# A first load of 64 KB rows, issued as a 2 KB strip of each row and then the other 62 KB

## Chip, cores, metric

One core of one Trainium2 chip. The metric is the device time of one execution in microseconds; the profile's span (first to last instruction of the program) is about 1.8 us shorter than that time. "Before" and "changed" are always compared on the same chip, in alternating rounds.

## The reference

The kernel turns 96 float32 images of 256 by 256 by 180 degrees. No arithmetic: each image's 65,536 elements come out in reverse order.

```python
def setup_inputs():
   batch, c, h, w = 32, 3, 256, 256
   return {"x": np.random.randn(batch, c, h, w).astype(np.float32)}

def reference(x: np.ndarray) -> np.ndarray:
   return np.rot90(x, k=2, axes=(-2, -1)).astype(np.float32)
```

## The kernel before

The 96 images are cut into three groups of 32, and each image into 4 pieces of 64 KB, so that a group fills a tile of 128 partitions by 64 KB. A load is one transfer of 128 rows of 64 KB. VectorE reverses each row inside SBUF (from tile A to tile C in four copies, or within tile B in twelve), and the store writes the four pieces of an image in reverse order. All transfers are issued by the sync engine, and they stand in one queue (q1, with all 864 packets of the page).

```python
    A = pool.tile([P, E], x.dtype, tag="A")        # E = 16384 elements, 64 KB
    Bt = pool.tile([P, E], x.dtype, tag="B")
    Ct = pool.tile([P, E], x.dtype, tag="C")
    T = pool.tile([P, J], x.dtype, tag="T")
    ...
    def load(t, g, lo=0, hi=E):
        nc.sync.dma_start(out=t[:, lo:hi], in_=x4[g][:, lo:hi])

    def store(t, g):
        nc.sync.dma_start(out=o4[g][:, ::-1, :], in_=t[:, :])

    def across(dst, src):
        for c in range(0, E, K):                   # K = E // 4
            copy(dst[:, c:c + K], back(src, E - c - K, E - c))
    ...
    load(A, 0)
    load(Bt, 1)
    across(Ct, A)
    store(Ct, 0)
    load(A, 2)
    inside(Bt)
    store(Bt, 1)
    across(Ct, A)
    store(Ct, 2)
```

Of the kernel before, what the change touches and what calls it, by code (L numbers as in the profile page):

```python
# [2 lines left out]

os.environ.setdefault("NEURON_RT_ULTRASERVER_MODE", "4")

# [4 lines left out]


@with_exitstack
def kernel(
    ctx: ExitStack,
    tc: tile.TileContext,
    x: bass.AP,
    out: bass.AP,
):








    nc = tc.nc
    P = 128

    B, C, H, W = x.shape
    L = H * W
    G = 32
    E = L // 4
    K = E // 4
    J = E // 8

    x4 = x.rearrange("b c h w -> (b c) (h w)").rearrange(
        "(g n) (s e) -> g (n s) e", n=G, s=4)
    o4 = out.rearrange("b c h w -> (b c) (h w)").rearrange(  # L40
        "(g n) (s e) -> g n s e", n=G, s=4)

    pool = ctx.enter_context(tc.tile_pool(name="slots", bufs=1))
    A = pool.tile([P, E], x.dtype, tag="A")
# [4 lines that stand above are left out]
    def back(t, lo, hi):  # L49
        return t[:, hi - 1:(lo - 1 if lo else None):-1]  # L50

    def copy(dst, src):
        tc.keep_in_program_order(nc.vector.tensor_copy(out=dst, in_=src))  # L53
# [8 lines that stand above are left out]
        for c in range(0, E, K):  # L62
            copy(dst[:, c:c + K], back(src, E - c - K, E - c))

    def inside(t):
        for lo in range(0, E // 2, J):
            hi = E - lo - J
            copy(T[:, :], back(t, hi, hi + J))
            copy(t[:, hi:hi + J], back(t, lo, lo + J))
            copy(t[:, lo:lo + J], T[:, :])  # L70

    load(A, 0)
    load(Bt, 1)
    across(Ct, A)
    store(Ct, 0)
# [7 lines that stand above are left out]
# [1 line left out]
_INS = ['x']  # L84
_OUTS = [((32, 3, 256, 256), 'float32')]


# [23 lines left out]
```

## Time and profile before

| | before |
|---|---|
| time, median of 3 runs | 123.19 us (123.14 to 123.35) |
| span in the profile | 121.3 us |
| share of the DMA queue | 97.3% |
| VectorE busy | 32.5 us |

The lines behind this table, and what they say, stand in the prediction. Some words for what follows: a transfer "lands" when the last of its 16 semaphore increments, one by each engine, has arrived (96 in the trace, for six transfers). The trace also has a record for each packet (start, duration, bytes), one packet for each row of a transfer and one for each increment; where I speak of "the packet records", the figures are worked out from those. The "loss" of a packet is the time that it takes over the steady duration of packets of its size (2.418 us for 64 KB), given per engine as a mean over the 16.

### The profile page before, as it was taken

Reading aid. Unit: us, or ns where it says so; the run is one execution under the profiler, and the core shown is the slowest. Engines: PE = TensorE matmul, PEld = TensorE weight load, DVE = VectorE, ACT = ScalarE, POOL = GpSimd, SP = SyncE. Lnnn points to the kernel's source line nnn. Section 1 sums busy time; section 2 is a strip of 40 time slices with the busy share of each in tenths; the row PEclk is TensorE's granted clock in tenths of the full one; section 3 lists DMA queues with packets and bytes.
Section 4 is the critical chain, followed back from the end, with each engine's and each line's share of the span. In section 5 each row is a group of like instructions: output and inputs, shape, how many; then the busy total and the mean of one; then the engine's idle time right before and its main releaser. Section 6 shows DMA issues by size and latency. Waiting matters only on the chain.

```text
span 121.3 us, 72 instructions
## 1 busy us (share of the span) xinstructions
DVE 32.5 (27%) x20; POOL 0.2 (0%) x4
## 2 busy tenths in 40 slices
DVE  0000000599300079999100000009990000000000
POOL 0000000000000000000000000000000000000000
DMA  9777977997899497799789977997798779877980
GB/s 346 346 346 346 692 346 346 389 649 346 346 432 605 195 497 346 346 605 432 346 346 605 432 346 346 627 411 346 346 649 389 346 346 649 389 346 346 670 368 0
DMA packets 864, 50.33 MB, mean 415 GB/s; under 512 B 96, under 2 KB 96, under 8 KB 96
## 3 DMA queue, kind: packets, MB, share of 16 engines
q1 hardware_dynamic: 864, 50.33, 97.3%
HBM read 25.17 MB, written 25.17 MB: 415 GB/s over the span
## 4 chain that ended last, share of the span: by engine, by line
DMA 59%; DVE 13%; DVEq 2%; SPq 1%; issue 0%
DMA A<-in_x_dram 59%; DVE Ct L53 13%; DVEq L106 2%; SPq L59 1%; DVEq L53 0%
## 5 line engine op out<-in xcount | busy, mean ns | idle before, releaser
L53 DVE COPY Ct<-A 128x4096 f32<-128x4096 f32 x8 | 17.8, 2288 | 46.3 <-DMA A<-in_x_dram 46.3
L53 DVE COPY T<-Bt 128x2048 f32<-128x2048 f32 x4 | 4.9, 1228 | 11.7 <-DMA Bt<-in_x_dram 11.6
L53 DVE COPY Bt<-Bt 128x2048 f32<-128x2048 f32 x4 | 4.9, 1227 | 0.1
L53 DVE COPY Bt<-T 128x2048 f32<-128x2048 f32 x4 | 4.9, 1226 | 0.1
L95 POOL MEMSET const-bfloat16-1.0<- 128x1 bf16 x1 | 0.1, 102 | 0.0
L95 POOL MEMSET const-uint8-127<- 128x1 uint8 x1 | 0.1, 101 | 0.0
L95 POOL MEMSET const-float32-0.0<- 128x1 f32 x1 | 0.1, 99 | 0.2 <-issue 0.2
L95 POOL MEMSET const-float32-1.0<- 128x1 f32 x1 | 0.1, 98 | 0.0
## 6 DMA issues: line engine op xcount, KB each, us to landing
A<-in_x_dram SPq DMA_DIRECT2D x2, 35.7
out_dram<-Ct SPq DMA_DIRECT2D x2, 30.3
Bt<-in_x_dram SPq DMA_DIRECT2D x1, 41.9
out_dram<-Bt SPq DMA_DIRECT2D x1, 42.9
```

The source lines that it names most:

```text
L53: tc.keep_in_program_order(nc.vector.tensor_copy(out=dst, in_=src))
L59: nc.sync.dma_start(out=o4[g][:, ::-1, :], in_=t[:, :])
L95: nc = _bacc.Bacc("TRN2", target_bir_lowering=False, num_devices=1)
L106: with _tile.TileContext(nc) as tc:
```

## The change

The intent, as far as the code tells it: a small piece first, so that something is there early.

```diff
+    N = E // 32
 ...
-    load(A, 0)
+    load(A, 0, 0, N)
+    load(A, 0, N, E)
     load(Bt, 1)
     across(Ct, A)
```

## The prediction

The forecast's sum came to +0.1 us: 0.05 for eight more packets per engine, 0.01 for one more semaphore packet, and 0.05 for a gap between strip and rest. This last term is cut in step 5 with its reason, which no trace here shows; it was the author's estimate. Without it the sum is +0.06 us, 123.25 in place of 123.3 us.

The 27.2 GB/s per engine and the 6 ns per packet, with which the text reckons, can be worked out from the records of before: a packet of 64 KB takes 2.4155 us from start to start and one of 4 bytes 6 ns, so the bytes alone need 2.4095 us, 27.2 GB/s. "Such packets", 96 of them, are those of 4 bytes, the semaphore increments (the page: 96 under 512 B).

> **What bounds the kernel now.** I read the page first: the busy shares, then the slices, then the queue. They show a core that moves data and does little else.
>
> ```profile
> span 121.3 us, 72 instructions
> DVE 32.5 (27%) x20; POOL 0.2 (0%) x4
> ...
> DMA  9777977997899497799789977997798779877980
> ...
> q1 hardware_dynamic: 864, 50.33, 97.3%
> HBM read 25.17 MB, written 25.17 MB: 415 GB/s over the span
> ```
>
> VectorE is busy a quarter of the span. The one DMA queue is busy 97.3% of it, so only 2.7% of 121.3 us, 3.3 us, is time in which the 16 engines have no packet. The slices swing between 7 and 9 because a packet is 64 KB and its bytes are booked at one moment; they are not idle time.
>
> Next, the chain of waits that ended last. It goes through the first load, the four copies of it, the issue of the store and of the third load, and then the third load's landing. It tells of semaphores and not of the queue: the 49.66 us "wait" for the third load is mostly that load standing in line behind the second load and the first store.
>
> ```profile
> 0.73 21.82 DMA A<-in_x_dram
> 22.55 0.02 issue
> 22.57 8.91 DVE Ct L53 x4
> ...
> 32.17 49.66 DMA A<-in_x_dram
> ```
>
> What shows whether the line ever runs dry is the timeline of the issuing engine, against the landings.
>
> ```profile
> 0.73 0.38 SPq L56 DMA_DIRECT2D A<-in_x_dram  x1
> 1.17 0.42 SPq L56 DMA_DIRECT2D Bt<-in_x_dram  x1
> 31.50 0.63 SPq L59 DMA_DIRECT2D out_dram<-Ct  x1
> 32.17 0.59 SPq L56 DMA_DIRECT2D A<-in_x_dram  x1
> 58.22 0.55 SPq L59 DMA_DIRECT2D out_dram<-Bt  x1
> 90.86 0.54 SPq L59 DMA_DIRECT2D out_dram<-Ct  x1
> ```
>
> ```profile
> DVE Ct L53 <- DMA A<-in_x_dram: 46.3, 2, 23.7
> DVE T L53 <- DMA Bt<-in_x_dram: 11.6, 1, 11.6
> ```
>
> Landings, worked out as issue plus time to landing: first load 0.73 + 21.82 = 22.55; second load 43.09 (VectorE begins on it then, after waiting 11.6 us); first store 31.50 + 31.1 = 62.6; third load 32.17 + 49.66 = 81.8; second store 58.22 + 42.9 = 101.1; last store 90.86 + 29.6 = 120.5. The first store was issued at 31.50 while the second load ran until 43.09, so it had 11.6 us in hand; the last store was issued at 90.86 and its turn came at 101.1, 10.2 us in hand. The queue never waits for VectorE. Each transfer is 8.39 MB, and the landings lie 20.5, 19.5, 19.2, 19.3 and 19.4 us apart.
>
> So the span is a sum: six transfers of about 19.33 us (116.0), plus a start of 22.55 - 19.33 = 3.2 us, plus 1.2 us that the second load takes more than the others, plus 121.3 - 120.5 = 0.8 us after the last landing: 121.2. Only the 3.2 and the 1.2 are not plain streaming.
>
> The trace's packet records give more of both. An engine takes eight 64 KB packets per transfer, one 2.418 us, and the next begins at the end of the one before (mean distance of starts in the middle of the trace: 2.4155 us). The first packets start between 1.74 and 2.70 us (mean 1.95) and end between 4.89 and 5.30 (mean 5.04), so they take 0.67 us more than a later one. Those that start early take up to 3.3 us, the two that start last 2.60: they end together, as if data flowed from about 2.5 us on for all. The other loss is in the last packet of the second load, just before the first store: 3.3 to 4.0 us instead of 2.418, mean loss 1.12. No later change of direction costs more than 0.02 us on average.
>
> [...] the stretch from 3 to 20 us shows 432 GB/s.
>
> ```profile
> 3.00:20.00 17.00, 0.00 (x0) 0.00 (x0) 1.00 1.00 432
> ```
>
> [...] At 27.2 GB/s per engine 65,536 bytes need 2.409 us; with 2.4155 measured, a packet costs 6 ns beside its bytes[...].
>
> [...] The trace has 96 such packets (6 transfers by 16 engines). In the records each takes 9 ns, and the next data packet starts 6 ns after it did[...].
>
> [...]
>
> **The change part by part.** Removed: one issue of 128 rows of 64 KB. Added: an issue of 128 strips of 2 KB and one of 128 rests of 62 KB. The bytes are the same. The static order of instructions shows the rest: the first copy of the first tile now waits for the long part, the fourth copy for the strip, and the third load waits for both; nothing else moves. VectorE's instructions keep their count and size.
>
> 1. Bytes: 0 us.
> 2. Packets: per engine 8 more, at 6 ns: 0.05 us. By rows: 8 x (2048 B / 27.2 GB/s + 6 ns) = 8 x 81 ns = 0.65 us for the strips, 8 x (63,488 B / 27.2 + 6 ns) = 8 x 2.340 = 18.72 for the rests, together 19.37 against 8 x 2.4155 = 19.32. This lies on the path, as everything in the queue does.
> 3. One more semaphore packet per engine: 6 to 9 ns, on the path.
> 4. One more issue on the sync engine: 0.38 to 0.42 us by the timeline, plus 0.06 between. It delays the issue of the rest to about 1.17 and of the second load to about 1.65. The second load has until 22 us, so for it nothing comes of this.
> 5. A gap between strip and rest. If the first packets flow from about 2.5 us, the strips are done at 2.5 + 0.65 = 3.15, for the last engine at about 3.5. The rest, issued 0.44 later than the strip, should have its first packets at 1.74 + 0.44 = 2.2 to 2.70 + 0.44 = 3.1. So they are there in time. [...]
> 6. The waits of VectorE: the long part lands last, at about 22.6, as the whole did; a delay of 0.1 us is eaten by the 11.6 us in hand.
> 7. The start itself: the strip meets the same first-packet delay of 0.67 us, and the rest doesn't pay it again if it is a delay of the first access. 0 us.
>
> Sum: 0.05 + 0.01 + 0.05 = about +0.1 us, a tenth of a per cent: 123.3 us.
>
> **The rivals.** A: small packets are not pipelined, and each strip pays a part of the 0.67 us that the first packet pays. Eight times 0.67 would be 5.4 us, 128.6 us, slower by 4%. Against it: everywhere after the first, packets follow each other without a gap, and the 9 ns semaphore packets too. For it: no data packet below 64 KB of this queue is in the trace. A mild form (0.1 us more per strip) gives +0.8 us, 124.1.
>
> B: the second issue has its own start-up, so that between strip and rest the engines stand still for up to a first-packet delay: +0.5 to +0.9 us, 123.8 to 124.1. For it: the strip is over in about 0.65 us, shorter than the 1.0 us from an issue's start to its first packet. Against it: the rest is issued only 0.44 us later.
>
> C: a gain. The early engines hold their first packet 0.7 us too long; if what delays them depends on the size of the first packet, short ones could hide it: up to -0.7 us, 122.5. Or the 1.12 us stall before the first store depends on how the engines stand to each other or on the count of packets before it, and the strip moves or removes it: 122.1. Against it: the engines' spread is the same after any split, and the first store comes at the same place in the order. Both together make 1.8 us, 1.5%, so even this rival stays within 2%; more than the 3.3 us without a packet plus the two stalls is not there to be won.
>
> D: the copies of the first tile start earlier, because part of the tile is there early. Ruled out by the order of waits: the first copy waits for the long part. Even if it did start earlier, the queue has no use for it.
>
> **Range and chances.** Working point 123.3. Downwards rival C in part, upwards rival B and the mild form of A; runs of one kernel agree within 0.2 us (123.14 to 123.35). Range 122.6 to 124.0. A gain over 2% needs 2.5 us, of which the profile shows no source: 0.01. A loss over 2% needs 0.31 us per strip, the strong rival A: 0.03. Within 2%: 0.96.
>
> **What would show it right or wrong.** In the changed trace: 864 + 128 + 16 = 1008 packets, the same MB; a span of about 121.4; the queue's share near 97%; landings still 19.2 to 19.5 us apart, with the second load's 1.2 extra still there; VectorE's wait for the second load near 11.6. Strips should take about 0.08 us each after the first, and the first long packets should start as the strips end. Wrong would be: strips of several tenths each (A), a stretch between 2.5 and 5 us in which the queue is idle (B), a first landing before 22.2 or a second load nearer to 19.3 (C).

## The result, and the profile after

Changed kernel: 122.98 us median of 4 runs (122.82 to 123.28), before 123.16 (123.02 to 123.35). The ratio is 0.9987 with a 95% interval of 0.9963 to 1.0011: the same. Later, on another chip with five rounds, the same pair gave 1.0008 (0.9996 to 1.0020).

The page of the changed kernel: the span, VectorE, the busy tenths of the DMA engines, the packets and the queue.

```profile
span 121.2 us, 75 instructions
DVE 32.5 (27%) x20; POOL 0.2 (0%) x4
...
DMA  9977987997899497799789977997798779877980
...
DMA packets 1008, 50.33 MB, mean 415 GB/s; under 512 B 112, under 2 KB 112, under 8 KB 240
...
q1 hardware_dynamic: 1008, 50.33, 97.4%
```

1008 packets are the 864 of before, 128 strips and 16 more semaphore increments (112 in place of 96); bytes, share and VectorE stand as before.

The chain of waits (start, duration, what). It has one piece more, the issue of the strip, and then goes the same way with the same lengths.

```profile
0.73 0.38 SPq L58
...
1.17 21.43 DMA A<-in_x_dram
...
22.63 8.91 DVE Ct L55 x4
...
32.31 49.42 DMA A<-in_x_dram
```

The timeline of the issuing engine and VectorE's waits. The second load is issued at 1.63 in place of 1.17 us; its turn comes at 22. VectorE has 11.5 us in hand before the second tile lands, before 11.6.

```profile
0.73 0.86 SPq L58 DMA_DIRECT2D A<-in_x_dram  x2
1.63 0.43 SPq L58 DMA_DIRECT2D Bt<-in_x_dram  x1
31.56 0.63 SPq L61 DMA_DIRECT2D out_dram<-Ct  x1
```

```profile
DVE Ct L55 <- DMA A<-in_x_dram: 46.3, 2, 23.7
DVE T L55 <- DMA Bt<-in_x_dram: 11.5, 1, 11.5
```

The issues with time to landing, in the changed kernel: the strip has landed 2.8 us after its issue, 19 us before the rest, and nobody asks for it then.

```profile
A<-in_x_dram SPq DMA_DIRECT2D x1, 7936.0 KB, 21.4
A<-in_x_dram SPq DMA_DIRECT2D x1, 256.0 KB, 2.8
```

The packet records show the start in detail. Each column is a mean over the 16 engines.

| | before | changed | changed, second profile |
|---|---|---|---|
| first long packet of an engine starts | 1.95 us | 2.94 | 2.85 |
| packets of the first 10 us: time over their steady duration, sum per engine | 0.67 | 0.57 | 0.52 |
| first packet of the second load starts | 21.95 | 21.92 | 21.95 |
| last packet of the second load: time over 2.418 us | 1.12 | 1.13 | 1.33 |
| last packet of all ends | 119.70 | 119.71 | 119.90 |

The third line is the balance of the change: nothing, within 0.03 us, which is less than the noise of that reading (below). The difference between the first and the second profile of the same kernel lies in the fourth line, which the change does not touch.

### The profile page after: what moved, and what is told of

It is laid out like the page before. It is cut to its first block, busy times and chain, and to the rows that moved or that the text cites. A ratio compares the mean times of both kernels' runs of the same rounds, so it can differ in the third digit from the quotient of the medians.

```text
span 121.2 us, 75 instructions
## 1 busy us (share of the span) xinstructions
DVE 32.5 (27%) x20; POOL 0.2 (0%) x4
## 2 busy tenths in 40 slices
DMA packets 1008, 50.33 MB, mean 415 GB/s; under 512 B 112, under 2 KB 112, under 8 KB 240
## 3 DMA queue, kind: packets, MB, share of 16 engines
q1 hardware_dynamic: 1008, 50.33, 97.4%
## 4 chain that ended last, share of the span: by engine, by line
DMA 58%; DVE 13%; DVEq 2%; SPq 1%; issue 0%
DMA A<-in_x_dram 58%; DVE Ct L55 13%; DVEq L109 2%; SPq L61 1%; SPq L58 0%; DVEq L55 0%
## 5 line engine op out<-in xcount | busy, mean ns | idle before, releaser
L55 DVE COPY T<-Bt 128x2048 f32<-128x2048 f32 x4 | 4.9, 1227 | 11.6 <-DMA Bt<-in_x_dram 11.5
```

The source lines that it names most:

```text
L55: tc.keep_in_program_order(nc.vector.tensor_copy(out=dst, in_=src))
```

## The experiments

All kernels were correct. An execution over 1.5% above the fastest of its kernel counts as slow and is left out of a ratio; there was one such in e5 (125.38 us, the fastest 123.04) and one in e6 (124.87, the fastest 122.77). The diffs that take out `load(A, 0, 0, N)` are against the changed kernel, that of e11 is against e6, and the others are against the kernel before.

| run | edit | median us, before beside it | ratio to before (95%) |
|---|---|---|---|
| after_again | the change | 123.17, 123.06 | 1.0008 (0.9996 to 1.0020) |
| e1_strip_last | strip after the rest | 123.24, 123.06 | 1.0018 (1.0001 to 1.0035) |
| e3_halves | two halves | 123.13, 123.06 | 1.0009 (0.9997 to 1.0021) |
| e2_32_strips | 32 strips | 125.17, 123.06 | 1.0167 (1.0154 to 1.0181) |
| e4_strip_64b | strip of 64 bytes | 123.59, 123.27 | 1.0005 (0.9965 to 1.0045) |
| e5_late_second | second load at 4.3 us | 123.20, 123.27 | 0.9990 (0.9943 to 1.0037) |
| e6_early_store | strip stored early, other queue | 122.93, 123.27 | 0.9955 (0.9916 to 0.9995) |
| e7_load_first | third load before first store | 122.92, 123.26 | 0.9976 (0.9958 to 0.9994) |
| e8_second_at_18 | second load at 18.6 us | 123.95, 123.26 | 1.0059 (1.0034 to 1.0084) |
| e9_8_strips | 8 strips | 123.14, 123.23 | 1.0003 (0.9983 to 1.0023) |
| e10_16_strips | 16 strips | 123.44, 123.23 | 1.0018 (1.0005 to 1.0031) |
| e11_store_between | strip stored between loads | 122.84, 123.23 | 0.9967 (0.9952 to 0.9981) |

Differences of 0.1 us cannot be read from these times; they are read from the packet records, which exist once per kernel. Kernels that start with the same undivided load (before, e5, e7, e8) begin their second load at 21.95, 21.87, 21.98 and 21.96 us; this, some 0.05 us to either side, is the noise of that reading.

### Is it the split, or the short packets in front?

The change once more; the strip last; two halves.

> The changed kernel again, for the noise of its trace and a narrower interval. Theory M: ratio 1.000 to 1.001. Rival C: ratio 0.998 to 0.999, and the start's loss again about 0.1 us smaller than before.

```diff
-    load(A, 0, 0, N)
-    load(A, 0, N, E)
+    load(A, 0, 0, E - N)
+    load(A, 0, E - N, E)
```

> The first load is split as in the change, but the 62 KB part of each row comes first and the 2 KB strip last, so the same 1008 packets and issues, with no short packet at the start. Theory M (mine: a split costs 6 ns a packet and a semaphore, about 0.06 us, and where the strip stands does not matter): within 0.1 us of the changed kernel, and the start of the trace loses its 0.67 us as before. Rival C (short first packets take part of the start's delay away, which gives back the 0.06): here the gain is gone, the second load begins 0.1 us later than in the changed kernel, at about 22.0 from the span's start, against 21.90 there and 21.95 before.

```diff
-    load(A, 0, 0, N)
-    load(A, 0, N, E)
+    load(A, 0, 0, E // 2)
+    load(A, 0, E // 2, E)
```

> The first load as two halves of 32 KB of each row: two transfers, but no short packet. Theory M: as the changed kernel, +0.06 us. Rival C (what helps at the start is that the first packets are short): the start's loss is nearer to the 0.67 us of before than to the 0.57 us that the changed kernel's records show.

Measured start of the second load: 21.95 us with the strip in front, 21.97 with the strip last, 21.85 with halves. Loss in the first 10 us: 0.52, 0.63 and 0.52. The first two agree with the theory that only the sum of bytes, packets and semaphores counts. The halves, with packets of 32 KB in front, have as small a loss as the strips, so a gain that only short packets bring is not seen. Over all the runs, the six kernels with 62 to 64 KB packets in front (or with 64 bytes before them) lose 0.60 to 0.68 us, the five with 2 KB or 32 KB in front 0.51 to 0.58, and the one with 8 KB 0.61 (those cut into 4 KB or 2 KB throughout lose 0.92 and 0.99, spread over several transfers). So 0.1 us may be there to be won, the smallest form of rival C, but it does not go by length, and the starts of the second load do not show it beyond their noise. No run settles whether it is real.

### Must the strip have a certain length?

Rival G has the long packets slow at the start whatever strip went before them.

```diff
-    load(A, 0, 0, N)
-    load(A, 0, N, E)
+    load(A, 0, 0, 16)
+    load(A, 0, 16, E)
```

> The strip is 64 bytes of each row in place of 2 KB. Its 8 packets per engine are over in under 0.2 us. Theory M (the delay at the start belongs to the first access, the rest does not pay it again): the long packets that follow lose next to nothing, the total is as in the changed kernel. Rival G [...]: the long first packets show 0.3 to 0.7 us over 2.41 each, as they did in the changed kernel (0.35), and the total is as before. Rival B (a gap because the strip is over before the rest is there): engines idle 0.2 to 0.5 us, second load begins at 22.1 to 22.4.

The chain of waits of this kernel: the whole first tile is there at 23.25 us, in the changed kernel at 22.61.

```profile
1.17 22.08 DMA A<-in_x_dram
23.25 0.02 issue
23.27 8.91 DVE Ct L55 x4
```

The records say why. The 64-byte packets take 8 to 11 ns each and lose nothing at all. Then the engines have nothing until the rest's first packets come, on average at 2.45 us, 0.50 us after an undivided load's would (1.95). Those long packets lose 0.65 us each, as if no strip had gone before. The second load begins at 22.42, 0.47 us later than before. So rival B's gap is real, and it fits the second issue: the rest is issued 0.44 us later, its packets come 0.50 us later, and the load ends as much later. In the changed kernel the 2 KB strips hold the engines for 0.99 us (0.65 at their steady pace and 0.34 of loss), which covers that time. And step 7 falls: the loss at the start is not a first access that a small packet can take on itself.

The whole-execution ratio, 1.0005, doesn't show the half microsecond: its interval is 0.4% to either side, and the runs of before in that batch ran from 122.98 to 124.55.

### Does the second load's issue slow the first packets?

The kernel before, with

```diff
+    nc.gpsimd.memset(Bt[:, 0:4096], 0.0)
     load(Bt, 1)
```

Of rival G this run tests one form: that the early issue of the second load slows the first packets.

> The kernel before, with one change: a memset on GpSimd of a quarter of the second tile makes the second load's issue late by several us (it has until 22 us). [...] Theory M (first access): the start's loss stays 0.67 us, the time is that of before. Rival G [...]: the first packets' mean excess falls from 0.67 to 0.3 us or less, and the time falls by as much, 0.3%.

The second load was issued at 4.27 us, and the first packets still lost 0.60 us (before: 0.67). So it is not the early issue of the second load that slows them. The first load was issued at 0.73 us as before, so whether its own issue slows them stays open.

The records hold a pattern that goes further. Add to the mean start of the first long packets their loss: that is the time from which they would have run at full pace.

| first long packets | issued | start | loss | full pace from |
|---|---|---|---|---|
| undivided load, or 62 KB first (before, e1, e5, e7, e8) | 0.73 us | 1.94 to 1.99 | 0.60 to 0.68 | 2.54 to 2.65 |
| behind a strip of 64 bytes (e4) | 1.17 | 2.45 | 0.65 | 3.10 |
| behind a strip of 2 KB (changed twice, e6, e11) | 1.17 | 2.85 to 2.94 | 0.23 to 0.31 | 3.16 to 3.18 |

The later the rest starts, the less it loses, and it comes to full pace at nearly the same time, some 0.5 us after an undivided load. It looks as if each long transfer had a delay of its own, counted from its issue (1.8 to 2.0 us from there to full pace); no run moved that issue alone, so this is not shown. It would explain the balance of the change: the rest is at full pace 0.54 us later than an undivided load (3.16 against 2.62), the strips have by then brought bytes that take 0.60 us at the steady rate, and the added packets cost about as much as the difference. Why a long transfer starts slowly, I did not find.

### The dose

32, 8 and 16 transfers in place of one.

```diff
-    load(A, 0, 0, N)
-    load(A, 0, N, E)
+    for lo in range(0, E, N):        # e9: 4 * N, e10: 2 * N
+        load(A, 0, lo, lo + N)
```

> The dose: the first load as 32 transfers of a 2 KB strip each, 256 packets per engine in place of 8, and 31 more semaphores. Theory M: 256 x 80 ns = 20.5 us + 31 x 6 ns = 0.2 against 19.3, so +1.3 us, all of it in the first load, the first landing of the whole tile at about 23.9; time about 1.1% above before. Rival A (short packets each pay a latency): several us more than that. Rival B (each transfer has a start of its own, a few tenths): 31 x 0.3 = +9 us. A third: the sync engine's issues, 32 x 0.44 = 14 us, would bind only if an issue took over 0.66 us.

> The first load as 8 transfers of 8 KB of each row, a dose between the changed kernel and the one with 32 strips, whose whole first load landed 2.99 us later, 96 ns for each of its 31 added transfers. Sum of the prediction (5 ns a packet, 6 a semaphore, both on the path): the first load lands 56 x 5 + 7 x 6 = 0.3 us later than before. By the measured 96 ns: 0.7 us later. And the 1.1 us before the first store: theory N (enough transfers before it take it away, 33 did) puts them anywhere between none and all; if they are gone at 8 transfers, the kernel is 0.4 us (0.3%) faster than before; theory T alone (the first turn from loads to stores always pays) leaves them, and e2 would stay unexplained.

> The first load as 16 transfers of 4 KB of each row. Sum of the prediction: 120 x 5 + 15 x 6 = 0.7 us; by the measured 96 ns per added transfer: 1.4 us later. Theory N: the 1.1 us at the first turn are smaller than with 8, or gone, and then the time is within 0.3% of before; theory T: they stay and the time is 0.6 to 1.2% above before.

The timeline of VectorE, in the kernel before and then with 32 transfers, with 8 and with 16: when it begins on the first tile, and when on the second.

```profile
22.57 8.90 DVE L53 COPY Ct<-A 128x4096 f32<-128x4096 f32 x4 [22.57 <-DMA A<-in_x_dram]
43.09 1.23 DVE L53 COPY T<-Bt 128x2048 f32<-128x2048 f32 x1 [11.62 <-DMA Bt<-in_x_dram]
```

```profile
25.66 8.90 DVE L55 COPY Ct<-A 128x4096 f32<-128x4096 f32 x4 [25.66 <-DMA A<-in_x_dram]
44.92 1.23 DVE L55 COPY T<-Bt 128x2048 f32<-128x2048 f32 x1 [10.36 <-DMA Bt<-in_x_dram]
```

```profile
23.07 8.90 DVE L55 COPY Ct<-A 128x4096 f32<-128x4096 f32 x4 [23.07 <-DMA A<-in_x_dram]
42.88 1.23 DVE L55 COPY T<-Bt 128x2048 f32<-128x2048 f32 x1 [10.90 <-DMA Bt<-in_x_dram]
```

```profile
23.98 8.90 DVE L55 COPY Ct<-A 128x4096 f32<-128x4096 f32 x4 [23.98 <-DMA A<-in_x_dram]
43.23 1.23 DVE L55 COPY T<-Bt 128x2048 f32<-128x2048 f32 x1 [10.36 <-DMA Bt<-in_x_dram]
```

Read each pair twice. The first line against 22.57 of the kernel before gives the cost: +0.5 us for 7 added transfers, +1.4 for 15, +3.1 for 31. With 32, about 0.1 us of it lies after the load: the last landing was at 25.54, and VectorE began at 25.66 (before: 22.55 and 22.57). The sum of the prediction gave 0.3, 0.7 and 1.3, so it was too small by 40 to 60%. By the records of the engines' own packets, the second load begins 0.26, 1.19 and 2.59 us later on the mean of the engines; there the sum holds for 8 transfers and fails for 16 and 32.

The steady distance of the landings' semaphore increments (mean over the engines) tells the term: a transfer of 8 packets per engine takes 2.487 us with 8 KB packets (2.409 of it bytes), 1.279 with 4 KB (1.205), and 0.679 with 2 KB (0.602). The bytes are reckoned at 27.2 GB/s per engine, which the trace of the halves shows too: a packet of 32 KB takes 1.213 us and one of 64 KB 2.418, that is 1.205 us for 32 KB more. Thus 0.074 to 0.078 us on each transfer beside its bytes; the prediction had 8 x 6 + 6 = 54 ns. The starts of the semaphore packets show that this isn't so from the beginning: up to about 14 us the transfers of all three kernels have stretches at 2.45, 1.25 and 0.65 us, some 45 ns beside their bytes, and only later the longer distance. Why it changes, no run here shows. For the one transfer that the change adds, either figure is within some 20 ns of the forecast, which is nothing. For 31 added ones 0.077 us each make 2.4 us, and some 0.3 us more are lost in the first 10 us (strips 1.0 us, before 0.67): about the 2.6 us by which the engines begin the second load later on their mean. The rest of the 3.1 is that they end further apart, and VectorE's 0.1.

Rival A is out: 256 strip packets per engine, at worst 12 ns each (3.1 us / 248 added), are not latencies of tenths. The static order and the timeline of the issuing engine with 32 transfers bring in one thing that I had not reckoned with: from the ninth transfer on, an issue waits for an earlier strip's semaphore, so the 32 issues spread over 19.74 us of the load itself (8 issues took 4.08 us, 16 took 13.24).

```profile
0.73 19.74 SPq L58 DMA_DIRECT2D A<-in_x_dram  x32
20.82 0.33 SPq L58 DMA_DIRECT2D Bt<-in_x_dram  x1
```

The second reading is the distance of the two lines. Before it is 20.52 us. Here it is 19.26 with 32 transfers, 19.81 with 8, 19.25 with 16. The 1.1 us that the second load loses at its end are gone with 16 and with 32 transfers, and partly with 8. In the records the loss in the last packet of the second load, before the first store, is 1.12 to 1.32 us (the first load as one transfer: before, e5, e8), 1.13 to 1.33 (as two), 0.68 (as eight), 0.02 (as sixteen and as thirty-two). That gave back 1.1 us of what the many transfers had cost, which is why 16 transfers are only 0.2% slower than one.

### What is lost before the first store?

Rival C had counted on this stall to move. First the early store, by the other issuing engine, of a strip that was loaded and copied first; `store` takes bounds and an issuing engine for it.

```diff
-    load(A, 0)
+    load(A, 0, E - N, E)
+    load(A, 0, 0, E - N)
     load(Bt, 1)
-    across(Ct, A)
-    store(Ct, 0)
+    copy(Ct[:, 0:N], back(A, E - N, E))
+    store(Ct, 0, 0, N, nc.scalar)
+    ...                              # the other copies
+    store(Ct, 0, N, E)
```

> About the 1.12 us that the last packets of the second load lose just before the first store, in both kernels. Here the strip is the one that becomes the first 2 KB of the output rows; it is copied and stored at once from the other issuing engine's queue, so that the core's first store happens at about 5 us; the remaining 62 KB are stored as before. Theory W (the first write of the execution to memory pays about a microsecond once): the 1.12 us are gone at 38.7 us; they come up at about 5 us instead, or are hidden there, and the kernel is up to 0.9% faster. Rival T (the turn from loads to stores in the queue pays it): they stay at 38.7 us, and the time is that of the changed kernel or some tenths more for the extra transfer.

The stall stayed at 39 us (1.17 us), though this core had written to the output since 7.8 us, so it is not the execution's first write to memory that pays. A surprise on the way, from the issues with time to landing:

```profile
out_dram<-Ct ACTq DMA_DIRECT2D x1, 256.0 KB, 23.9
```

256 KB took 23.9 us. The records show that each engine did one 2 KB packet of this store, then one 62 KB packet of the load, and so on: the store packets of an engine start 2.42 us apart. Here the two queues took turns by packets, though one packet was 31 times as long as the other.

Then the third load before the first store, so that the turn from loads to stores comes one transfer later.

```diff
-    store(Ct, 0)
     load(A, 2)
+    store(Ct, 0)
```

> About the 1.12 us that every kernel but the one with 32 strips lost in the last packet before its first store from the sync engine's queue. The kernel before, with the third load issued just before the first store (it waits for the same copies), so that the second load is followed by a load and the turn to stores comes one transfer later. Theory T (the turn from loads to stores pays): no loss at 38.7 us, but about 1.1 us at about 58 to 61 us. Theory I (what pays is the last packet of the transfers that were issued at the very start and had been long in the queue, whatever follows): the 1.1 us stay at 38.7 us. Either way the time is that of before within 0.3%.

VectorE's timeline in this kernel, the starts on the first and on the second tile:

```profile
22.69 8.90 DVE L53 COPY Ct<-A 128x4096 f32<-128x4096 f32 x4 [22.69 <-DMA A<-in_x_dram]
42.04 1.23 DVE L53 COPY T<-Bt 128x2048 f32<-128x2048 f32 x1 [10.45 <-DMA Bt<-in_x_dram]
```

The distance is 19.35 us in place of 20.52: the second load loses nothing, and the packets from 58 us on lose 1.04 us, just before the store that now comes there. The stall moved with the first turn from loads to stores. Theory T is right about the place here.

Then the second load held back until its turn had nearly come.

```diff
+    for _ in range(5):
+        nc.gpsimd.memset(Bt[:, 0:4096], 0.0)
     load(Bt, 1)
```

> The kernel before, with the second load held back by memsets of its tile until about 18 us (its turn in the queue comes at 22 us). With 32 strips the second load was issued at 20.8 us and the 1.12 us were gone. Theory I (a transfer that has lain in the queue for long, with nothing issued after it for 30 us, pays at its end): they are gone here too, and the kernel is 0.9% faster, about 122.1 us. Theory N (it is the count of transfers that went before, 33 there and 2 to 3 elsewhere) and theory T (the turn): they stay at 38.7 us, and the time is that of before.

It was issued at 18.55 us, and the records still show 1.26 us lost before the first store. Theory I is out: a late issue does not save the second load, and with 16 transfers it was issued earlier, at 14.92 us, and lost nothing. This kernel came out 0.6% slower than before; its engines end further apart (the increments of the last store's semaphore spread over 1.05 us, before 0.69), and why that is I did not follow.

Last, the strip's store in the same queue, between the first and the second load.

```diff
-    load(Bt, 1)
     copy(Ct[:, 0:N], back(A, E - N, E))
-    store(Ct, 0, 0, N, nc.scalar)
+    store(Ct, 0, 0, N)
+    load(Bt, 1)
```

> As the early store of a 2 KB strip, but from the same queue as everything else, between the rest of the first load and the second load. So the queue turns from loads to stores at about 22 us, for 2 KB packets. Theory T (the first turn of this queue pays 1.1 us): the loss comes up at about 20 to 22 us and is gone at 39 us. If it is the first turn to long stores that pays, it stays at 39 us, and 22 us shows nothing. No gain in time over the changed kernel either way.

It was neither: 0.17 us lost before the short store at 22 us, and 0.90 still lost before the long one at 39 us. Theory T, as I stated it, fails here: the first turn does not pay it all. Together with the dose it leaves this: the loss comes just before the first long store of this queue, is smaller when the first load is cut into 8 transfers, and is gone with 16. In those kernels the packets become shorter and more numerous along with the transfers (64 per engine with 8, 128 with 16, against 8), so which of the two counts is untested. By what mechanism, no run here shows.

This last kernel has the lowest median of all, 0.3% below before, with a clear interval; the early store and the third load first are 0.2 to 0.5% below as well. None of the three removes the stall (0.90 to 1.17 us are still lost), and the ends of their last packets, 119.62 to 119.72 us against 119.70 before, do not show where the gain would come from. I call none of them an improvement worth the code.

## Why the prediction was right

The time, the share and the count of packets came as forecast: 123.3 us forecast, 122.98 measured, and the change is within noise. The mechanism, a full queue in which a split costs only the overhead of its packets, is borne out; one of its zeros, step 7, was right by luck. By its steps:

1. Bytes: 50.33 MB in both. Right.
2. Packets: strips start 80 ns apart in the steady stretch of the kernel that stores a strip between loads, long packets of the changed kernel 2.340 us apart; forecast 81 ns and 2.340 us. Right for single packets. For whole short transfers the dose shows some 45 ns early in the load and 74 to 78 later, where the sum had 54: near enough for this change, too small for 16 and 32 transfers.
3. The semaphore packet takes 9 ns, all 112 of them, as in the kernel before. Right.
4. The issue: second load at 1.63 us, forecast 1.65. Right, and without effect.
5. The gap: small, as forecast (0.05 us), with long packets starting as the strips end (2.57 to 3.43 us). The 64-byte strip shows when the rest can start: 2.21 to 3.00 us, forecast 2.2 to 3.1. The strips held the engines until 2.94 on average, so there was half a microsecond in hand. Rival B was right that the second issue's packets come with a delay of their own; the length of the strip hides it.
6. VectorE: 11.5 us in hand, forecast 11.6. Right.
7. The start: this step failed. It said that the strip meets the 0.67 us of the first access and that the rest does not pay again. In the changed kernel the strips lost 0.34 us and the first long packets 0.23 (second profile 0.21 and 0.31); behind a 64-byte strip, which lost nothing, the long packets lost the full 0.65. The total came out near the forecast, 0.52 to 0.57 us against 0.67, so the zero stands while its reason does not. By the table above it stands because the strips moved bytes while the rest came to full pace 0.54 us late; that the two cancel within 0.1 us is luck, as far as the prediction goes.

In sum +0.1 us was forecast at the second load's start, and 0.0 with some 0.05 us of noise measured. Rival A is refuted by the dose. Rival C's gain at the start is at most 0.1 us and not told from noise; its other half, that the stall could be removed by what comes before it, is possible as 16 transfers show, but one strip more is far too little. Rival D is settled by the trace as by the order: the strip lay there from 3.5 us on and the first copy began at 22.63.

## What to carry to other kernels

In this kernel one queue is busy 97.3% of the span, and splitting a transfer in two moved the start of the next one by 0.03 us at most and the time by nothing that shows (ratios 0.9987 and 1.0008). So look first for whether the queue is ever empty, and for the transfers in hand. The place where this split could cost was the start: here the first piece had to keep the engines busy for the half microsecond until the second issue's packets came, or the difference was lost (0.47 us with 64 bytes, nothing with 2 KB). And ask of a small early piece whether an instruction waits for that piece alone, and whether what bounds the kernel profits; here the first copy waited for the long part until 22.63 us, and the bound was the queue, at 97.4%.
